# An MLP's up-projection as seven block products in place of eight, and its two halves split at DRAM

## The chip, the cores and the metric

The kernel runs on one core of one Trainium2 chip (trn2). TensorE (PE) multiplies, VectorE (DVE), ScalarE (ACT) and GpSimd (POOL) work on rows, and SyncE (SP) issues the transfers between DRAM and the on-chip memory SBUF. Products land in PSUM, in banks of 128 partitions x 512 float32. The metric is the time of one execution on the device, in microseconds (us).

## The reference, cut to what matters

```python
for i in range(DEPTH):                       # DEPTH = 2 layers
    ...                                      # four attention groups, h = h + mix @ w_o[i]
    hn = rms_norm(h, ffn_norm[i])            # 1024 tokens x 1024
    u = dwconv_centred(hn @ w_up[i], conv_w[i], conv_b[i])   # 1024 x 5632, 3 taps along the tokens
    gate, val = jnp.split(u, 2, axis=-1)
    h = h + (jax.nn.gelu(gate) * val) @ w_down[i]            # 2816 -> 1024
    e = p[i] @ w_ple_proj[i]
    g = jax.nn.sigmoid(rms_norm(h, ple_norm[i]) @ w_ple_gate[i])
    h = h + g * e
```

## The kernel before, in words

Every large product is made in three matmuls: both operands are split into a high part (a cast to the matmul's own float format, `hi`) and the rest (`lo`), and hi·hi, hi·lo and lo·hi are added up in PSUM (`products`, `mm3`, `mm_side`; the matmuls themselves are recorded at line L181). A split costs one cast and one subtraction over the same elements.

Per layer, around the change:

- **The projection stage** (`proj`, `turn`, `emb`), for each of 8 blocks of 128 tokens: the last half of the output projection is added to h, the rows are normed, transposed and split into `xh`/`xl` (two halves of 512 tokens), and e is made and stored to DRAM. All eight blocks of h stay in SBUF.
- **The MLP loop.** The 5632 columns of w_up lie in 44 tiles of 128; tile f (gate) and tile 22 + f (value) make one of the 22 activations. `up_tile` makes one tile: 48 matmuls 128x512 into `psS`, a pair of PSUM banks (two such pairs exist), then the three taps of the convolution straight out of PSUM (L1124 on ACT, L1125 and L1126 on DVE). `act_tile` calls it twice, puts gelu (L1133, ACT) and the product gate x value (L1135, POOL) behind it, and splits the result into `ah`/`al` (L1138 ACT, L1139 DVE). Activations never leave SBUF.
- Two activations make one chunk of the down-projection: `down_tile`, for each of the 8 token blocks, 12 matmuls into the two banks `psM(0)` and `psM(1)` and two additions to h on DVE (L1197). Eleven chunks. While chunk ch runs, the up tiles of chunk ch + 1 are made: a scheduler orders the instructions of each engine, and puts up matmuls between the down tiles.
- In the last layer (`last`) a down tile runs its two halves one after the other (`outs[:1]`, then `outs[1:]`); in the first layer it alternates between them.
- The last chunk of a layer (`down_last`) runs in a pipeline with the norm and the gate stage behind it. Its second activation is made in pieces by `act_last`.

Weights come as float32 tiles through `WRing.piece`: a transfer of 512 KB, and the split on POOL (L111 high part, L112 low part). Each engine works through its own queue in order; semaphores join them.

Of the kernel before, what the change touches and what calls it, by code (L numbers as in the profile page):

```python
# [19 lines left out]
P = 128  # L20
# [25 lines left out]
def kernel(ctx: ExitStack, tc: tile.TileContext, a, out, dbg=None):  # L46
# [992 lines left out]
    for L in range(DEPTH):  # L1039
# [10 lines left out]
        stg = c0.enter_context(tc.tile_pool(name="stg", bufs=2))  # L1050
        gp = c0.enter_context(tc.tile_pool(name="gp", bufs=1))
        hp = c0.enter_context(tc.tile_pool(name="hp", bufs=1))
        h = [hp.tile([P, D], F32, name=f"h{t}") for t in range(NT)]
        xF = [(xp.tile([P, KD, 512], F32R, name=f"xh{i}"), xp.tile([P, KD, 512], F32R, name=f"xl{i}"))
              for i in range(2)]

        with ExitStack() as c:
            mp = c.enter_context(tc.tile_pool(name="mp", bufs=2))
            np_ = c.enter_context(tc.tile_pool(name="nrm", bufs=2))
            ringe = WRing(c, "e", 6, 0, stage=ring.s)  # L1060
            ep = c.enter_context(tc.tile_pool(name="es", bufs=2))
            W = [ring.piece(a["w_o"][L, k * P:(k + 1) * P, :], 1024, pool=False) for k in (2, 3)]
            gB = load_gB(gp, a["ffn_norm"][L])
            Pt = [ringe.piece(a["p"][L, k * P:(k + 1) * P, :], 1024, pool=k == 0) for k in range(2)]
            We = {}

            def emb(i):
                n, t = i // NT, i % NT
                cs = slice(n * 512, (n + 1) * 512)
                if t == 0:  # L1070
                    We[n] = ringe.piece(a["w_ple_proj"][L, :, cs], 1024, 2)
                tf = slice(t * P, (t + 1) * P)
                e = psT(i)
                mm3(e, [((Pt[k][0][:, tf], Pt[k][1][:, tf]),
                         (We[n][0][:, k * 512:(k + 1) * 512], We[n][1][:, k * 512:(k + 1) * 512])) for k in range(2)])
                es = ep.tile([P, 512], F32, name="es", tag="es")
                se.copy(es, e)
                nc.sync.dma_start(ed[t][:, cs], es)

            def proj(t, _):  # L1080
                nc.sync.dma_start(h[t], hpart[t])
# [5 lines left out]
                for n in range(2):  # L1087
                    o = psM(n)
                    cs = slice(n * 512, (n + 1) * 512)
                    mm3(o, [((mh[:, k], ml[:, k]), (W[k][0][:, cs], W[k][1][:, cs])) for k in range(2)])  # L1090
                    ve.tensor_tensor(h[t][:, cs], o, h[t][:, cs], op=ALU.add)
                return norm_a(np_, h[t], gB)

            def turn(t, hn):
                tk = slice((t % 4) * P, (t % 4 + 1) * P)
                norm_b(hn, xF[t // 4][0][:, :, tk], xF[t // 4][1][:, :, tk], t if t < 4 else 1)
                emb(2 * t)
                emb(2 * t + 1)
# [4 lines left out]
        ap_ = cf.enter_context(tc.tile_pool(name="act", bufs=5))  # L1103
        kp = cf.enter_context(tc.tile_pool(name="cw", bufs=1))
        cw = kp.tile([P, 2 * NF, 4], F32, name="cw")
        nc.sync.dma_start(cw, a["conv"][L])
        cu = ExitStack()
        up_ = cu.enter_context(tc.tile_pool(name="up", bufs=2))

        def up_mm(f, dst):  # L1110
            hi, lo = ring.piece(a["w_up"][L, f], 1024)
            outs = [(dst[n], [((hi[:, k * P:(k + 1) * P], lo[:, k * P:(k + 1) * P]), (xF[n][0][:, k], xF[n][1][:, k]))
                              for k in range(KD)]) for n in range(2)]
            if last:
                for o, pairs in outs:
                    mm3(o, pairs, by_pass=True)
            else:
                mm_side(outs)

        def up_tile(f):  # L1120
            s = psS(0 if f < NF else 1)
            up_mm(f, (s[:, :512], s[:, 512:]))
            u = up_.tile([P, S], F32, name="u", tag="ug" if f < NF else "uv", bufs=2 if f < NF else 1)
            se.activation(u, s, AF.Identity, bias=cw[:, f, 3:4], scale=cw[:, f, 1:2])  # L1124
            ve.scalar_tensor_tensor(u[:, 1:], s[:, :S - 1], cw[:, f, 0:1], u[:, 1:], op0=ALU.mult, op1=ALU.add)  # L1125
            ve.scalar_tensor_tensor(u[:, :S - 1], s[:, 1:], cw[:, f, 2:3], u[:, :S - 1],  # L1126
                                    op0=ALU.mult, op1=ALU.add)
            return u

        def act_tile(f):  # L1130

            g = up_tile(f)
            se.activation(g, g, AF.Gelu_apprx_tanh)  # L1133
            v = up_tile(NF + f)
            ge.tensor_tensor(v, g, v, op=ALU.mult)  # L1135
            hi = ap_.tile([P, S], F32R, name="ah", tag="act")
            lo = ap_.tile([P, S], F32R, name="al", tag="act")
            se.copy(hi, v)  # L1138
            ve.tensor_tensor(lo, v, hi.bitcast(F32), op=ALU.subtract)  # L1139
            return lambda t: (hi[:, t * P:(t + 1) * P], lo[:, t * P:(t + 1) * P])  # L1140

        def act_last(f):

            g = up_tile(f)
            se.activation(g, g, AF.Gelu_apprx_tanh)
            f += NF
            s = (psT(0), psT(1))
            up_mm(f, s)
            cut = 384
            A = up_.tile([P, S], F32, name="u", tag="uv", bufs=1)[:, :cut]  # L1150
            B = up_.tile([P, S], F32, name="u", tag="ug", bufs=2)[:, :S - cut]

            def tap(u, o, src, j):
                ve.scalar_tensor_tensor(u[:, o:o + src.shape[1]], src, cw[:, f, j:j + 1],
                                        u[:, o:o + src.shape[1]], op0=ALU.mult, op1=ALU.add)

            def split(u, lo_):
                n = u.shape[1]
                ve.tensor_tensor(u, g[:, lo_:lo_ + n], u, op=ALU.mult)
                if lo_ == 0:  # L1160
                    x = ap_.tile([P, S], F32R, name="ahl", tag="act")
                    hi, lo = x[:, :n], x[:, n:2 * n]
                else:
                    hi = ap_.tile([P, S], F32R, name="ah", tag="act")[:, :n]
                    lo = ap_.tile([P, S], F32R, name="al", tag="act")[:, :n]
                se.copy(hi, u)
                ve.tensor_tensor(lo, u, hi.bitcast(F32), op=ALU.subtract)
                return hi, lo

            b, w = cw[:, f, 3:4], cw[:, f, 1:2]  # L1170
            se.activation(A, s[0][:, :cut], AF.Identity, bias=b, scale=w)
            tap(A, 1, s[0][:, :cut - 1], 0)
            tap(A, 0, s[0][:, 1:cut + 1], 2)
            pa = split(A, 0)
            m = 512 - cut
            se.activation(B[:, :m], s[0][:, cut:], AF.Identity, bias=b, scale=w)
            se.activation(B[:, m:], s[1], AF.Identity, bias=b, scale=w)
            tap(B, 0, s[0][:, cut - 1:511], 0)
            tap(B, m, s[0][:, 511:], 0)
            tap(B, m + 1, s[1][:, :511], 0)  # L1180
            tap(B, 0, s[0][:, cut + 1:], 2)
            tap(B, m - 1, s[1][:, :1], 2)
            tap(B, m, s[1][:, 1:], 2)
            pb = split(B, cut)

            def get(t):
                (hi, lo), o = (pa, t * P) if t * P < cut else (pb, t * P - cut)
                return hi[:, o:o + P], lo[:, o:o + P]
            return get

        def down_tile(t, acts, W):
            halves = [(psM(n), slice(n * 512, (n + 1) * 512)) for n in range(2)]
            outs = [(o, [(x(t), (wh[:, cs], wl[:, cs])) for x, (wh, wl) in zip(acts, W)]) for o, cs in halves]
# [5 lines left out]
        NC_ = NF // 2  # L1199
        pend = [act_tile(0), act_tile(1)]  # L1200
        for ch in range(NC_):
            W = [ring.piece(a["w_down"][L, f * P:(f + 1) * P, :], 1024) for f in (2 * ch, 2 * ch + 1)]
            cur = pend
            if ch + 1 == NC_:
                break
            pend = [act_tile(2 * ch + 2)]
            for t in range(NT):
                down_tile(t, cur, W)
            pend.append((act_last if ch + 2 == NC_ else act_tile)(2 * ch + 3))
        cu.close()  # L1210


        xt_cm.__exit__(None, None, None)
# [26 lines left out]
        with ExitStack() as c:  # L1240
# [5 lines left out]
            def down_last(t, _):  # L1246
                down_tile(t, cur, W)
# [108 lines left out]
```

## Time and profile before

| | before |
|---|---|
| median of 3 runs | 3514.02 us (3509.81 to 3517.78) |
| the profiled execution | 3509.35 us |
| its span, first to last instruction | 3507.3 us |
| mean granted clock of TensorE | 0.982 |
| PE busy | 3330.8 us, 95% of the span |
| DVE, ACT, POOL busy | 48%, 31%, 32% |

The span lies 2 us below the profiled execution's own time, and that execution 4.7 us below the median. A row of the profile gives an engine's busy time, a share of the span or the time of one instruction; a matmul's own duration overlaps the next one's, so the pace of a run of matmuls is read from the starts.

### The profile page before, as it was taken

The page shows a single profiled execution, that of the slowest core. Times are in us where ns is not written, and L with a number is a line of the kernel's source. Part 1 is how long each engine was busy: PE and PEld are TensorE (multiplying, and loading weights), DVE is VectorE, ACT ScalarE, POOL GpSimd, SP SyncE. Part 2 cuts the span into 40 slices and gives each one's busy share as a digit, 9 for nine tenths or more (in the row PEclk, how much of TensorE's full clock was granted, in tenths as well). Part 3 has the DMA queues.
Part 4 walks back from the last instruction along what each step waited for, and adds up shares of the span by engine and source line. Part 5 has one row for each costly group of instructions (what it writes and reads, how often), then busy time and mean ns, then how long its engine had stood idle before and what let it go on. Part 6 is the DMA issues. An engine that isn't in the chain of part 4 may idle for free.

```text
span 3507.3 us, 49133 instructions
## 1 busy us (share of the span) xinstructions
PE 3330.8 (95%) x19616; PEld 2762.2 (79%) x19616; DVE 1673.3 (48%) x2496; ACT 1103.0 (31%) x2188; POOL 1107.0 (32%) x1060
## 2 busy tenths in 40 slices
PE   8999889997999999999999998899979999999998
PEld 8888778775777777777998887777757888888888
DVE  5676346544333333335647763565442333333354
ACT  3554357533211111112225543564332111111122
POOL 1532213202333433442415332131033344343331
PEclk9999989998999999999999999999989999999999
DMA  6211322324211111111322113223242111111112
GB/s 195 82 55 53 101 82 79 111 80 156 79 48 37 57 46 42 55 48 39 125 97 65 54 53 105 82 79 116 76 157 79 43 54 44 47 48 48 49 50 95
DMA packets 170835, 264.09 MB, mean 75 GB/s; under 512 B 33008, under 2 KB 121968, under 8 KB 170608
## 3 DMA queue, kind: packets, MB, share of 16 engines
q1 hardware_dynamic: 170608, 260.96, 23.4%
q8 instruction: 155, 2.54, 0.3%
q14 instruction: 72, 0.59, 0.1%
HBM read 200.80 MB, written 63.77 MB: 75 GB/s over the span
## 4 chain that ended last, share of the span: by engine, by line
PE 77%; issue 6%; DVE 5%; POOL 5%; ACT 3%; DMA 3%; SPq 1%; POOLq 0%; ACTq 0%; DVEq 0%
PE psS L181 30%; PE psM L181 29%; PE psT L181 4%; PE psT L256 3%; PE psM L264 2%; POOL wlo L112 2%; PE psM L580 2%; PE psS L700 1%; PE psS L422 1%; DVE Prow L428 1%; PE psT L890 1%; DVE nm L279 1%; ACT Prow L281 1%; POOL whi L111 1%; PE psS L161 1%
## 5 line engine op out<-in xcount | busy, mean ns | idle before, releaser
L111 POOL TENSOR_SCALAR whi<-wst 128x1024 fp32r<-128x1024 f32 (+2 forms) x194 | 212.6, 1096 | 1105.6 <-PE psM L181 558.7
L112 POOL TENSOR_TENSOR wlo<-wst,whi 128x1024 fp32r<-128x1024 f32 (+2 forms) x194 | 480.2, 2475 | 51.2 <-PE psS L181 38.5
L1125 DVE SCALAR_TENSOR_TENSOR u<-psS,cw,u 128x1023 f32<-128x1023 f32 x86 | 110.3, 1283 | 619.1 <-ACT u L1124 619.1
L181 PE MATMUL psS<-xl,whi 128*128 128x512 f32 x1376 | 396.7, 394 | 0.0
L181 PE MATMUL psS<-xh,whi 128*128 128x512 f32 x1376 | 393.3, 394 | 0.0
L181 PE MATMUL psS<-xh,wlo 128*128 128x512 f32 x1376 | 390.2, 394 | 0.0
L1124 ACT ACTIVATE u<-psS,cw 128x1024 f32<-128x1024 f32 x86 | 104.0, 1209 | 873.1 <-PE psS L181 873.1
L181 PE MATMUL psM<-whi,xh 128*128 128x256 f32 (+1 forms) x1408 | 370.3, 301 | 0.1
L181 PE MATMUL psM<-whi,xl 128*128 128x256 f32 (+1 forms) x1408 | 360.7, 295 | 2.3 <-DVE xl L163 2.3
L181 PE MATMUL psM<-wlo,xh 128*128 128x256 f32 (+1 forms) x1408 | 358.1, 293 | 3.9 <-POOL wlo L112 3.9
L1197 DVE TENSOR_TENSOR h<-psM,h 128x512 f32<-128x512 f32 x352 | 235.2, 687 | 214.7 <-PE psM L181 214.7
L181 PEld LDWEIGHTS psS<-xh,wlo 128*128 128x128 f32 x1376 | 257.4, 187 | 63.5
L181 PEld LDWEIGHTS psS<-xl,whi 128*128 128x128 f32 x1376 | 257.4, 187 | 63.5
L181 PEld LDWEIGHTS psS<-xh,whi 128*128 128x128 f32 x1376 | 257.4, 187 | 62.9
L281 ACT ACTIVATE Prow<-psS,nm 128x1024 f32<-128x1024 f32 x192 | 214.4, 1118 | 195.8 <-DVE nm L279 195.3
L181 PE MATMUL psM<-whi,ah 128*128 128x512 f32 x692 | 264.6, 403 | 1.2 <-DVE h L1197 1.2
L181 PE MATMUL psM<-wlo,ah 128*128 128x512 f32 x692 | 256.4, 391 | 0.0
L181 PE MATMUL psM<-whi,al 128*128 128x512 f32 x692 | 255.9, 391 | 0.0
L181 PEld LDWEIGHTS psM<-whi,xh 128*128 128x128 f32 x1408 | 248.3, 193 | 7.9 <-ACT pr_raw L232 4.3
L279 DVE TENSOR_REDUCE nm<-psS 128x1 f32<-128x1024 f32 x192 | 230.5, 1216 | 47.6 <-PE psS L422 29.4
L181 PEld LDWEIGHTS psM<-wlo,xh 128*128 128x128 f32 x1408 | 248.5, 193 | 5.5 <-POOL wlo L112 5.4
L181 PEld LDWEIGHTS psM<-whi,xl 128*128 128x128 f32 x1408 | 248.9, 194 | 3.3 <-DVE xl L163 3.2
(276 smaller groups left out, 6001.9 us busy)
## 6 DMA issues: line engine op xcount, KB each, us to landing
wst<-w_up SPq DMA_DIRECT2D x88, 512.0 KB, 3.5
wst<-w_down SPq DMA_DIRECT2D x44, 512.0 KB, 3.3
wst<-w_in SPq DMA_DIRECT2D x36, 512.0 KB, 3.7
wst<-w_o SPq DMA_DIRECT2D x16, 512.0 KB, 4.4
hp<-o_hx SPq DMA_DIRECT2D x16, 512.0 KB, 2.6
h<-hp SPq DMA_DIRECT2D x16, 512.0 KB, 5.7
e<-es SPq DMA_DIRECT2D x32, 256.0 KB, 2.5
wst<-w_ple_gate SPq DMA_DIRECT2D x16, 512.0 KB, 3.5
```

The lines of the kernel that those rows point to most:

```text
L111: ge.tensor_scalar(hi, src, 1.0, 0.0, op0=ALU.mult, op1=ALU.add)
L112: ge.tensor_tensor(lo, src, hi.bitcast(F32), op=ALU.subtract)
L161: te.transpose(t[:, j], src[:, (c + j) * P:(c + j + 1) * P], ident)
L181: te.matmul(o, *ms[i], start=i == 0, stop=i == n - 1)
L256: te.transpose(t[:, i], src[:, (4 * c + i) * P:(4 * c + i + 1) * P], ident)
L264: te.matmul(o[z, :256], V(kt), PT[:, kt], start=(kt < 2), stop=(kt >= 6))
L279: ve.tensor_reduce(nm, s, op=ALU.max, axis=AX.X, negate=True)
L281: se.activation(p_, s, AF.Exp, bias=nm[:, 0:1], scale=1.0, accum_out=ssum)
L580: te.matmul(o[64 * j:64 * j + 64, g], V(2 * g + j, b), pt(2 * g + j, b), start=(b == 0), stop=(b == nb - 1))
L1124: se.activation(u, s, AF.Identity, bias=cw[:, f, 3:4], scale=cw[:, f, 1:2])
L1125: ve.scalar_tensor_tensor(u[:, 1:], s[:, :S - 1], cw[:, f, 0:1], u[:, 1:], op0=ALU.mult, op1=ALU.add)
L1197: ve.tensor_tensor(h[t][:, cs], o, h[t][:, cs], op=ALU.add)
```

## The change

The up-projection of one gate tile and its value tile is one product of a 2x2 block matrix of weights (gate and value by the two halves of the 1024 inputs; a11, a12, a21, a22) with a 2x2 block matrix of rows (b11, b12, b21, b22: the two halves of the inputs by the two halves of the tokens). It is made by Strassen's scheme in its form with fifteen additions: seven block products of 12 matmuls 128x512 in place of eight. The sums of the weights (s1 to s4) are made on POOL for each f, those of the rows (t1 to t4) once per layer in the projection stage. Three PSUM banks take the products: A is `psT`, B and C are the two halves of one `psS`. The results G and V are put together in SBUF by seven evictions, and the taps of the convolution read them there. The activation v goes to DRAM. When all 22 are done, h (stored to DRAM by the projection stage) is loaded again, and the down-projection runs alone: v is loaded, split and multiplied, in both layers with the two halves alternating. `act_last` is gone.

```diff
-        ring = WRing(c0, "f", 10, 2)
+        ring = WRing(c0, "f", 8, 4)
+        XC = ("b11", "b21", "b22", "t1", "t2", "t3", "t4")
...
-            def proj(t, _):
-                nc.sync.dma_start(h[t], hpart[t])
+            def proj(i, _):
+                t = tok(i)
+                ht = row_tile("h")
+                nc.sync.dma_start(ht, hpart[t])
...
+                nc.sync.dma_start(hd1[t], ht)
+                hn = row_tile("hn")
+                norm_rows(ht, gB, hn)
...
+                def split(name, src, e):
+                    hi, lo = (x[:, :, tk] for x in xc[name])
+                    se.copy(hi, src)
+                    e.tensor_tensor(lo, src, hi.bitcast(F32), op=ALU.subtract)
+                es = row_tile("es")
...
+                    ve.tensor_tensor(t1, b12, f[:, :4], op=ALU.subtract)
+                    ve.tensor_tensor(t2, s[:, 4:], t1, op=ALU.subtract)
+                    split("t2", t2, ge)
...
+        ap_ = c0.enter_context(tc.tile_pool(name="act", bufs=7))
+        sp_ = cu.enter_context(tc.tile_pool(name="wsum", bufs=4))
...
+        ORDER = (("a11", "b11", 0), ("s2", "t2", 1), ("a12", "b21", 0), ("s3", "t3", 1), ("s1", "t1", 2),
+                 ("a22", "t4", 1), ("s4", "b22", 2))
...
+                wsum(f, "s1", stat[f, "a21"], stat[f, "a22"], ALU.add)
+                wsum(f, "s2", stat[f, "s1"], stat[f, "a11"], ALU.subtract)
...
+            src = stat[f, ORDER[p][0]]
+            w = ring.w.tile([P, 1024], F32R, name="whl", tag="wp")
+            hi, lo = w[:, :512], w[:, 512:]
+            se.copy(hi, src)
+            (ve if p % 2 else ge).tensor_tensor(lo, src, hi.bitcast(F32), op=ALU.subtract)
...
+        def conv(f, u, x, half=None):
+            if half != 1:
+                se.activation(u, x, AF.Identity, bias=cw[:, f, 3:4], scale=cw[:, f, 1:2])
+                ve.scalar_tensor_tensor(u[:, 1:], x[:, :S - 1], cw[:, f, 0:1], u[:, 1:], op0=ALU.mult, op1=ALU.add)
+            if half != 0:
+                ve.scalar_tensor_tensor(u[:, :S - 1], x[:, 1:], cw[:, f, 2:3], u[:, :S - 1],
+                                        op0=ALU.mult, op1=ALU.add)
...
+            ge.tensor_tensor(v, g, v, op=ALU.mult)
+            nc.sync.dma_start(vd[f], v)
...
+        def act_load(f):
+            v = ring.s.tile([P, 1024], F32, name="wst")
+            nc.sync.dma_start(v, vd[f])
+            hi, lo = act("ah", F32R), act("al", F32R)
+            se.copy(hi, v)
+            ve.tensor_tensor(lo, v, hi.bitcast(F32), op=ALU.subtract)
...
+            s = psS(f)
+            banks = psT(f), s[:, :512], s[:, 512:]
...
+                multiply(f, p, banks)
+                if p == 0:
+                    se.copy(V[:, :512], A)
+                elif p == 1:
+                    ve.tensor_tensor(G[:, 512:], B, V[:, :512], op=ALU.add)
+                elif p == 2:
+                    se.copy(G[:, :512], A)
+                elif p == 3:
+                    ve.tensor_tensor(V[:, 512:], B, V[:, :512], op=ALU.add)
+                elif p == 4:
+                    ve.tensor_tensor(V[:, 512:], C, V[:, 512:], op=ALU.add)
...
+        for t in range(NT):
+            nc.sync.dma_start(h[t], hd1[t])
...
-            for z in ([outs[:1], outs[1:]] if last else [outs]):
-                mm_side(z)
+            mm_side(outs)
             for o, cs in halves:
                 ve.tensor_tensor(h[t][:, cs], o, h[t][:, cs], op=ALU.add)
...
+        for ch in range(NC_ - 1):
+            for t in range(NT):
+                down_tile(t, ch)
+                if t in (0, 2):
+                    act_load(2 * ch + 2 + t // 2)
+                elif t in (1, 3):
+                    down_w(2 * ch + 2 + t // 2)
```

The first place is DVE's queue in the up-projection. Before, in the steady part of the first layer, it held for each up tile two taps out of `psS`, and for each activation one subtraction for `al`:

```order
L1125 SCALAR_TENSOR_TENSOR u<-psS,cw,u 128x1023 [waits Activation_49]
L1126 SCALAR_TENSOR_TENSOR u<-psS,cw,u 128x1023 [waits DVE_49]
L1139 TENSOR_TENSOR al<-u,ah 128x1024 [waits Activation_49]
```

Now the queue holds for one f, from one L1198 to the next, the taps of the f before (`ug`, `uv`), the low parts of weights (`whl`, L1182) and the evictions of this f (L1245 after product 1, L1249 after 3, L1251 after 4, L1253 after 5, L1255 after 6):

```order
L1198 SCALAR_TENSOR_TENSOR ug<-G,cw,ug 128x1023 [waits Activation_49]
L1245 TENSOR_TENSOR G<-psS,V 128x512 [waits PE_49]
L1200 SCALAR_TENSOR_TENSOR ug<-G,cw,ug 128x1023 [waits DVE_49]
L1198 SCALAR_TENSOR_TENSOR uv<-V,cw,uv 128x1023 [waits Activation_49]
L1200 SCALAR_TENSOR_TENSOR uv<-V,cw,uv 128x1023 [waits DVE_49]
L1182 TENSOR_TENSOR whl<-wsum,whl 128x512 [waits PE_49,Activation_49]
L1249 TENSOR_TENSOR V<-psS,V 128x512 [waits DMAHW4_49,PE_49]
L1251 TENSOR_TENSOR V<-psS,V 128x512 [waits DVE_49,PE_49]
L1182 TENSOR_TENSOR whl<-wst,whl 128x512 [waits DMAHW5_49,Activation_49]
L1253 TENSOR_TENSOR V<-psS,V 128x512 [waits PE_49]
L1255 TENSOR_TENSOR G<-psS,G 128x512 [waits PE_49]
```

The taps have moved from PSUM to SBUF sources, and three of them and a low part now stand between the eviction L1245 and the eviction L1249.

PE's queue around the same eviction, in the same f: the end of product 3 (`t3`), four matmuls of the next f's product 0 (`b11`), and the start of product 4 (`t1`), whose wait is on L1249:

```order
L1193 MATMUL psS<-t3h,whl 128x512 x2
L1193 MATMUL psS<-t3l,whl 128x512
L1193 MATMUL psS<-t3h,whl 128x512
L1193 MATMUL psT<-b11h,whl 128x512 [waits Activation_49]
L1193 MATMUL psT<-b11l,whl 128x512
L1193 MATMUL psT<-b11h,whl 128x512 [waits Pool_49]
L1193 MATMUL psT<-b11h,whl 128x512
L1193 MATMUL psS<-t1h,whl 128x512 [waits DVE_49]
```

Product 4 goes to the other bank of the same `psS` tile that L1249 reads, and the wait is for the tile. Products 5 and 6 wait in the same way for L1251 and L1253, product 5 behind four matmuls of `b11`, product 6 behind four more.

The second place is PE's queue in the down-projection, at the border of two down tiles. Before, in the first layer, three matmuls of an up tile (`psS`) stood there:

```order
L181 MATMUL psM<-whi,ah 128x512 x2
L181 MATMUL psM<-wlo,ah 128x512 x2
L181 MATMUL psM<-whi,al 128x512 x2
L181 MATMUL psS<-xh_9318,whi 128x512
L181 MATMUL psS<-xh_9320,whi 128x512
L181 MATMUL psS<-xl_9319,whi 128x512
L181 MATMUL psM<-whi,ah 128x512 [waits DVE_49]
L181 MATMUL psM<-wlo,ah 128x512
```

Now, in both layers:

```order
L181 MATMUL psM<-whi,ah 128x512 x2
L181 MATMUL psM<-wlo,ah 128x512 x2
L181 MATMUL psM<-whi,al 128x512 x2
L181 MATMUL psM<-whi,ah 128x512 [waits DVE_49]
L181 MATMUL psM<-wlo,ah 128x512
L181 MATMUL psM<-whi,al 128x512
L181 MATMUL psM<-whi,ah 128x512 [waits DVE_49]
```

The matmul that waits for the addition to h now stands straight behind the last one of the tile before.

The third place is DVE's queue at the end of a chunk (h_13110 is block 6, h_13111 block 7, h_13104 block 0 of the next chunk). Before, one `al` stood there. Now there are two, which wait for matmuls of block 7 (`PE_49`), since the pool `act` has seven tiles for the eight that two chunks hold:

```order
L1285 TENSOR_TENSOR h_13110<-psM,h_13110 128x512 [waits DVE_49,PE_49] x2
L1229 TENSOR_TENSOR al<-wst,ah 128x1024 [waits DMAHW0_49,PE_49,Activation_49]
L1229 TENSOR_TENSOR al<-wst,ah 128x1024 [waits DMAHW4_49,DVE_49,DMAHW5_49,PE_49,Activation_49]
L1285 TENSOR_TENSOR h_13111<-psM,h_13111 128x512 [waits DVE_49,PE_49] x2
L1285 TENSOR_TENSOR h_13104<-psM,h_13104 128x512 [waits DVE_49,PE_49] x2
```

Both `al` have moved ahead of the additions of block 7.

## Rows read from the trace of the kernel before

**Rows 1.** The page: the engines' busy time, and the chain's shares by line.
```profile
PE 3330.8 (95%) x19616; PEld 2762.2 (79%) x19616; DVE 1673.3 (48%) x2496; ACT 1103.0 (31%) x2188; POOL 1107.0 (32%) x1060
PE psS L181 30%; PE psM L181 29%; PE psT L181 4%; PE psT L256 3%; PE psM L264 2%; POOL wlo L112 2%; PE psM L580 2%; PE psS L700 1%; PE psS L422 1%; DVE Prow L428 1%; PE psT L890 1%; DVE nm L279 1%; ACT Prow L281 1%; POOL whi L111 1%; PE psS L161 1%
```

**Rows 2.** Windows: projection stage, one chunk of layer 0, one of layer 1.
```profile
core 0: us, PE busy (x) PEld busy (x) DVE busy (x) ACT busy (x) POOL busy (x), PEclk, DMA share, GB/s
842.00:904.00 62.00, 52.00 (x245) 39.77 (x246) 32.92 (x35) 24.32 (x44) 28.64 (x29) 0.97 0.48 163
...
979.50:1047.30 67.80, 67.80 (x289) 53.38 (x289) 23.74 (x27) 9.05 (x8) 26.25 (x15) 1.00 0.14 45
...
2727.00:2793.70 66.70, 66.70 (x290) 53.88 (x289) 24.11 (x27) 9.05 (x8) 26.31 (x15) 1.00 0.15 47
```

**Rows 3.** The chain that ended last, layer 0, one chunk: start, us, what.
```profile
987.33 0.70 PE psS L181 x3
...
1001.75 39.90 PE psS L181 x171
```

**Rows 4.** The same chain, layer 1.
```profile
2727.02 17.70 PE psM L181 x78
```

**Rows 5.** Timeline of PE at a border of two down tiles, layer 0.
```profile
983.14 0.62 PE L181 MATMUL psM<-whi,al 128*128 128x512 f32 x2
983.59 0.63 PE L181 MATMUL psS<-xh,whi 128*128 128x512 f32 x2
...
984.31 0.51 PE L181 MATMUL psM<-whi,ah 128*128 128x512 f32 x1
```

**Rows 6.** Timeline of DVE at that border and the next.
```profile
983.57 1.29 DVE L1197 TENSOR_TENSOR h<-psM,h 128x512 f32<-128x512 f32 x2 [1.97 <-PE psM L181]
987.14 1.29 DVE L1197 TENSOR_TENSOR h<-psM,h 128x512 f32<-128x512 f32 x2 [2.29 <-PE psM L181]
```

**Rows 7.** Groups by line and shape: xcount | busy us, mean ns.
```profile
L1197 DVE TENSOR_TENSOR h<-psM,h 128x512 f32<-128x512 f32 x352 | 235.2, 687 | 214.7 <-PE psM L181 214.7
L1125 DVE SCALAR_TENSOR_TENSOR u<-psS,cw,u 128x1023 f32<-128x1023 f32 x86 | 110.3, 1283 | 619.1 <-ACT u L1124 619.1
L450 POOL TENSOR_TENSOR c_ob<-oh,gsub 128x512 f32<-128x512 f32 x8 | 10.3, 1288 | 0.6
L1135 POOL TENSOR_TENSOR u<-u 128x1024 f32<-128x1024 f32 x42 | 100.5, 2394 | 59.1 <-DVE u L1126 59.1
L1124 ACT ACTIVATE u<-psS,cw 128x1024 f32<-128x1024 f32 x86 | 104.0, 1209 | 873.1 <-PE psS L181 873.1
L1077 ACT COPY es<-psT 128x512 f32<-128x512 f32 x32 | 18.4, 583 | 11.9 <-DMA e<-es 7.1 <-ACT es L1077 2.5 <-PE psT L181 2.2
L658 DVE TENSOR_TENSOR a_sl<-a_x,a_sh 128x512 fp32r<-128x512 f32 x16 | 11.0, 688 | 3.4 <-ACT a_sh L657 2.9 <-DMA a_V<-A 0.5
```

**Rows 8.** Timelines of POOL and DVE: `al` beside POOL's split, and alone.
```profile
1001.35 3.24 POOL L112 TENSOR_TENSOR wlo<-wst,whi 128x1024 fp32r<-128x1024 f32 x1
...
1005.69 2.39 POOL L112 TENSOR_TENSOR wlo<-wst,whi 128x1024 fp32r<-128x1024 f32 x1
...
1000.24 2.10 DVE L1139 TENSOR_TENSOR al<-u,ah 128x1024 fp32r<-128x1024 f32 x1 [0.99 <-PE psM L181]
...
1026.78 1.23 DVE L1139 TENSOR_TENSOR al<-u,ah 128x1024 fp32r<-128x1024 f32 x1 [3.65 <-ACT ah L1138]
```

**Rows 9.** The chain ahead of the last chunk, layer 0.
```profile
1628.93 0.03 issue
...
1633.36 1.41 PE psM L181 x5
```

**Rows 10.** The page: DMA issues, KB each, median us to landing.
```profile
hp<-o_hx SPq DMA_DIRECT2D x16, 512.0 KB, 2.6
h<-hp SPq DMA_DIRECT2D x16, 512.0 KB, 5.7
```

**Rows 11.** The longest wait in the projection stage, layer 0: us, times, longest.
```profile
ACT xh L162 <- PE psS L161: 26.5, 7, 10.1
```

More of the change, by code (lines that the diff above doesn't have):

```diff
@@ L1048 @@
         c0 = ctx.enter_context(ExitStack())
-        ring = WRing(c0, "f", 10, 2)
[L1050 to L1055, printed above, removed]
+        ring = WRing(c0, "f", 8, 4)
@@ L1062, with row_tile @@
             W = [ring.piece(a["w_o"][L, k * P:(k + 1) * P, :], 1024, pool=False) for k in (2, 3)]
             gB = load_gB(gp, a["ffn_norm"][L])
-            Pt = [ringe.piece(a["p"][L, k * P:(k + 1) * P, :], 1024, pool=k == 0) for k in range(2)]
+            Pt = [ring.piece(a["p"][L, k * P:(k + 1) * P, :], 1024, pool=k == 0) for k in range(2)]
             We = {}
-            def emb(i):
-                n, t = i // NT, i % NT
+            def row_tile(name):
+                return np_.tile([P, D], F32, name=name, tag="row")
@@ new lines, in multiply @@
+        def multiply(f, p, banks):
+            hi, lo = stat.pop((f, p))
+            _, x, z = ORDER[p]
+            xh, xl = xc[x]
+            ms = products([((hi[:, k * P:(k + 1) * P], lo[:, k * P:(k + 1) * P]), (xh[:, k], xl[:, k]))
+                           for k in range(4)])
+            first = [o[2] for o in ORDER].index(z) == p
+            for i, m in enumerate(ms):
+                te.matmul(banks[z], *m, start=first and i == 0, stop=i == len(ms) - 1, skip_group_check=True)
+        def conv(f, u, x, half=None):
[5 more added lines that the diff above has]
+                                        op0=ALU.mult, op1=ALU.add)
@@ new lines, in down_w @@
+        def down_w(f):
+            Ws[f] = ring.piece(a["w_down"][L, f * P:(f + 1) * P, :], 1024)
+        for f in range(NF):
+            s = psS(f)
+            banks = psT(f), s[:, :512], s[:, 512:]
+            A, B, C = banks
+            G, V = act("G"), act("V")
+            for p in range(7):
+                multiply(f, p, banks)
+                if p == 0:
+                    se.copy(V[:, :512], A)
[7 more added lines that the diff above has]
+                    ve.tensor_tensor(V[:, 512:], C, V[:, 512:], op=ALU.add)
+                elif p == 5:
+                    ve.tensor_tensor(V[:, :512], B, V[:, :512], op=ALU.add)
+                else:
+                    ve.tensor_tensor(G[:, 512:], C, G[:, 512:], op=ALU.add)
+                if f + 1 < NF:
+                    prep(f + 1, p)
+                elif p in (1, 2):
+                    down_w(p - 1)
+                elif p in (4, 5):
+                    act_load(p - 4)
+                if p == 0 and f + 2 < NF:
+                    raw_load(f + 2)
+                next(rest, None)
+            rest = hidden(f, G, V)
@@ L1101 @@
+        for _ in rest:
+            pass
+        cu.close()
+        xt_cm.__exit__(None, None, None)
+        stg = c0.enter_context(tc.tile_pool(name="stg", bufs=2))
+        gp = c0.enter_context(tc.tile_pool(name="gp", bufs=1))
+        hp = c0.enter_context(tc.tile_pool(name="hp", bufs=1))
+        h = [hp.tile([P, D], F32, name=f"h{t}") for t in range(NT)]
+        for t in range(NT):
+            nc.sync.dma_start(h[t], hd1[t])
         cf = ExitStack()
         np_ = cf.enter_context(tc.tile_pool(name="nrm", bufs=2))
-        ap_ = cf.enter_context(tc.tile_pool(name="act", bufs=5))
@@ L1104 @@
[L1104 to L1118, printed above, removed]
@@ L1142, in act_last @@
[L1142 to L1189, printed above, removed]
```

132 lines of the change are left out of this document (84 added, 48 removed).

## The prediction

> **What bounds the kernel now.** I read the page's busy times first, then the chain that ended last, then windows cut at the chain's own period, then timelines inside one period. TensorE is busy for 95% of the span, and the two matmul lines of the MLP make most of the chain [rows 1]. The window of one chunk shows PE busy for all of it in either layer, at a granted clock of 1.00, while DVE works some 24 us of 67 and POOL 26 [rows 2]. So in the MLP every matmul taken out is worth its pace, as long as no new wait appears, and every wait put on PE costs its length.
>
> The pace comes from the chain, which joins matmuls that follow each other without a gap. Up-projection: 39.90 us for 171, 0.2333 us each [rows 3]. Down-projection in layer 1, with halves one after the other: 17.70 us for 78, 0.2269 us [rows 4]. The down tiles of layer 0 need a closer look. Three up matmuls, 0.70 us, stand between two tiles [rows 3]. The last pair of a tile starts at 983.14, the addition to h starts at 983.57 and takes 1.29 us for two halves, so the first half is free at about 984.2, and the next tile's first matmul starts at 984.31 [rows 5, 6]. PE was ready for it at 983.59, when it started the first of the three fillers [rows 5]. The eviction therefore costs a wait of 0.72 us, and the fillers hide it, no more and no less. In layer 1 the second half's matmuls hide it, which is why that layer needs no fillers.
>
> **Part 1, the up-projection.** One f takes 7 x 12 = 84 matmuls in place of 2 x 48 = 96. At 0.2333 us that is 19.6 us in place of 22.4; over 22 f 431 in place of 493 us; for two layers a gain of **123 us**. This is the ceiling.
>
> Added are weight sums and low parts on POOL (eight 128x512 operations at 1.29, one product at 2.39: 12.7 us per f), seven casts, two copies, two taps and a gelu on ACT (nine at 0.58 and three at 1.2: 8.8), and on DVE four taps, three low parts and five additions (4 x 1.23, 3 x 0.69, 5 x 0.69: 10.4 us) [rows 7, 8]. None reaches 19.6, so no engine's sum becomes the bound. The order does: product 4 waits for L1249, in front of which stand three taps and a low part, after L1245, which has to wait for product 1.
>
> Count from the end of product 6. Product 1 ends 12 matmuls later, at 2.8; L1245 at 3.5; three taps of 1.23 to 7.2; the low part to 7.9. L1249 also needs product 3, at 8.4, so it would be done at 9.15, and product 4, which PE reaches at 40 matmuls or 9.33, would not wait. That holds if each DVE step takes its time alone. The trace speaks against it. `al` has two SBUF inputs, and took 2.10 beside POOL's split and 1.23 alone; POOL's L112 took 3.24 and 2.39 [rows 8]. They shut each other out: both ends lie later by about the other's piece. Before, the taps read PSUM and kept 1.283 us over all 86 [rows 7]. Now they, too, have two SBUF inputs, and POOL is at work two thirds of the time. One or two collisions with a 1.29 us operation, or the product of 2.39 us against the low part (both are released by the fourth tap), put L1249's end at 10.5 to 13. Bounds for the wait per f: 0, and 4.1 (each of the four steps loses a whole 1.29 us operation: 7.9 + 5.2 + 0.7 = 13.8, less 9.33, less some that POOL hasn't ready). Products 5 and 6 have four fillers, 0.93 us, to hide an eviction of 0.69 and its semaphores (0.72 above), so they wait little. I take **1.6 us per f**, nearer to the lower bound because the collisions before L1245 cost nothing: 44 x 1.6 = +70, bounds 0 and +180.
>
> The Trainium skill has the rule behind this in "SBUF — State Buffer", section "Who interferes with whom": a DVE instruction with two SBUF inputs and a GpSimd instruction that reads SBUF want the same port pair, and the second to come is blocked until the first ends; one with at most one SBUF input doesn't contend. It speaks against moving the taps from PSUM to SBUF; the durations above agree with it. Without it this term would be 0, with it +70.
>
> **Part 2, the down-projection alone.** Nothing is left to fill the 0.72 us. The period from one tile's additions to the next was 983.57 to 987.14, 3.57 us, fillers included [rows 6]; the chain last matmul, addition, next tile's first matmul doesn't contain the fillers, so it stays at 3.57 without them. Before, the chunk's own matmuls cost 67.80 - 192 x 0.2333 = 23.0 us in layer 0 and 66.70 - 44.8 = 21.9 in layer 1 [rows 2]. Now 8 x 3.57 = 28.6. Ten chunks each (the last runs between the norm and gate stages as before): 56 + 67 = **+123 us**, bounds +110 and +130. What was saved in part 1 is given back here.
>
> At the end of each chunk two subtractions for `al` stand on DVE ahead of block 7's additions. They wait for matmuls of block 7 and for the casts, and the weight splits on POOL are released by the same matmuls. Alone they hold the additions up by about one operation, 1.23, less some slack; shut out by POOL twice (2.10 as in [rows 8], and more against 2.39) by up to 4.5. Lower bound 0.4. I take **2.5 us**, twice the duration alone: 20 chunk ends, +50, bounds +8 and +90. The transfers of v and the weights (four of 512 KB in 29 us, a few us each [rows 10]) are asked for a chunk ahead and are hidden.
>
> **The borders.** Between up and down, h has to be loaded: a transfer of 512 KB lands in 2.6 to 5.7 us [rows 10], the first addition needs one, and two tiles can't run ahead of it: +3 per layer, bounds 0 and 6. At the end `act_last` is gone: in the chain before, PE stood from 1628.93 to 1633.36 for its taps [rows 9]: -4.4 per layer. Together -3.
>
> **The projection stage.** It took 62.0 us, PE busy for 52 [rows 2], and the longest of its waits is ACT's for the transposes, 26.5 us, which PE doesn't feel [rows 11]. Added per pair of blocks: four differences and five more splits of 512 columns, and five shared row buffers in place of eight h and two hn, so that a block's h and sums wait for earlier stores. The matmuls stay. The extra DVE work is some 16 operations of 0.69, 11 us, on 33; POOL's 16 low parts of 1.29, 21 us, on 29 [rows 2, 7]. Below: hidden, 0. Above: POOL's and half of DVE's come on top, +30. I take **+15** per layer, +30.
>
> **Sum.** -123 + 70 + 123 + 50 - 3 + 30 = +147, on the profiled execution's 3509: 3656; against the median, which lies 5 us higher, **3661 us**.
>
> **Rivals.**
> - *The ports bind the up loop* (chance 0.14). Each tap loses a POOL operation: wait near 4.1 per f, +110 over mine, about 3770. For it: POOL's 65% busy share. Against: POOL's product waits for the fourth tap, so POOL is idle for part of the stretch.
> - *The up loop runs at its matmuls' pace* and only the down part waits (0.14): 3661 - 70, about 3590. For it: the walk without collisions ends 0.2 us before PE needs the bank.
> - *An even exchange* (0.06): only the 0.72 us wait is real, `al` and the projection stage hide: 3514 - 123 + 123, about 3514.
> - *PE finds the banks free* (0.06, the other side): DVE keeps up wherever PE asks. Place: the border of two down tiles and the border of products 3 and 4; price: 123 + 70 + 50 less; result some 3420. It decides if an eviction ends within the time that PE needs to come back to its bank; at the down border that time is nothing and the eviction 0.65 us, so little speaks for it.
> - Mine: 0.60. That the seven products don't save 12 matmuls per f is ruled out by the order.
>
> **How the numbers follow.** The bounds of the terms, added as independent ones (70, 42, 30 and 12 down; 110, 40, 30 and 10 up), give 3661 - 88 and + 121. The range reaches a little past the low rival at 3590 and to the port rival: **3555 to 3780**; it leaves out the last two rivals and the tails, 0.2. My own case alone: 3600 to 3725. A difference of 0.2%, 7 us, is what a measurement here can tell from no change. Faster: 0.06 and a share of the even exchange, 0.08; same 0.03; slower 0.89.
>
> **What the profile after would show.** PE's busy share in the up windows under 1, with PE waiting for DVE L1249, a period of 20.5 to 22 us per f, and taps with means over 1.23. In the down windows a period near 3.57 per tile with PE waiting for L1285, about 31 us per chunk, the longest wait of a chunk at its end behind L1229. No up matmul in the down part. The prediction is wrong if down tiles follow each other in under 3 us, if L1249 is done before PE gets there, or if the projection stage takes over 95 us.

## The result, and the profile after

The changed kernel takes **3665.64 us** (median of 4 runs, 3657.91 to 3667.94) against 3514.51 for the kernel before: a ratio of 1.0427, 95% interval 1.0408 to 1.0447. The profiled execution's span is 3656.1 us at a mean granted clock of 0.971; before it was 3507.3 at 0.982. So 148.8 us have to be found between the two spans.

The page's part on busy time answers to [rows 1]: PE does 528 matmuls fewer (12 for each of the 44 f), 37 us of busy time less, and its share falls from 95% to 90%.

```profile
PE 3293.3 (90%) x19088; PEld 2668.5 (73%) x19088; DVE 1975.8 (54%) x2874; ACT 1352.4 (37%) x2630; POOL 1349.0 (37%) x1262
```

What PE waits for, in all and in the whole span (engine and line, whom for, us, times, longest us):

```profile
PE psM L181 <- DVE h L1285: 134.5, 160, 5.6
PE psS L1108 <- DVE t L1131: 26.4, 6, 4.8
PE psS L1193 <- DVE V L1249: 26.2, 40, 1.1
...
PE psS L1193 <- DVE whl L1182: 10.0, 2, 5.0
```

The first row is the down-projection, the third the up-projection, the second the projection stage, and each is a place that the change made. Windows of four f of the up-projection and of one chunk of the down-projection, both layer 0, answer to [rows 2]:

```profile
core 0: us, PE busy (x) PEld busy (x) DVE busy (x) ACT busy (x) POOL busy (x), PEclk, DMA share, GB/s
987.49:1070.45 82.96, 80.37 (x337) 62.24 (x336) 45.58 (x48) 34.63 (x48) 54.36 (x37) 1.00 0.23 77
1452.24:1482.79 30.55, 24.22 (x96) 17.39 (x97) 13.39 (x19) 2.10 (x2) 8.76 (x5) 1.00 0.21 69
```

An f takes 82.96 / 4 = 20.74 us; a chunk, 96 matmuls in either kernel, takes 30.55 where the chunk before spent 23.0 and 21.9 us on it. The granted clock is 1.00 in both windows, as before. Timelines of the three engines show the two waits themselves, first in the up-projection, then at the end of a chunk:

```profile
1030.70 1.32 POOL L1159 TENSOR_TENSOR wsum<-wst 128x512 f32<-128x512 f32 x1 [0.70 <-POOL whl L1182]
1032.67 1.59 POOL L1182 TENSOR_TENSOR whl<-wst,whl 128x512 fp32r<-128x512 f32 x1 [0.65 <-ACT whl L1181]
1038.01 2.69 POOL L1212 TENSOR_TENSOR uv<-ug,uv 128x1024 f32<-128x1024 f32 x1 [3.74 <-DVE uv L1200]
...
1031.24 1.87 DVE L1198 SCALAR_TENSOR_TENSOR ug<-G,cw,ug 128x1023 f32<-128x1023 f32 x1 [0.67 <-ACT ug L1197]
1033.03 0.68 DVE L1245 TENSOR_TENSOR G<-psS,V 128x512 f32<-128x512 f32 x1
1033.63 1.72 DVE L1200 SCALAR_TENSOR_TENSOR ug<-G,cw,ug 128x1023 f32<-128x1023 f32 x1
1035.27 1.27 DVE L1198 SCALAR_TENSOR_TENSOR uv<-V,cw,uv 128x1023 f32<-128x1023 f32 x1
1036.58 1.28 DVE L1200 SCALAR_TENSOR_TENSOR uv<-V,cw,uv 128x1023 f32<-128x1023 f32 x1
1037.78 0.68 DVE L1182 TENSOR_TENSOR whl<-wsum,whl 128x512 fp32r<-128x512 f32 x1
1038.38 0.68 DVE L1249 TENSOR_TENSOR V<-psS,V 128x512 f32<-128x512 f32 x1
...
1039.12 0.50 PE L1193 MATMUL psS<-t1h,whl 128*128 128x512 f32 x1 [0.65 <-DVE V L1249]
...
1478.84 3.20 DVE L1229 TENSOR_TENSOR al<-wst,ah 128x1024 fp32r<-128x1024 f32 x2 [1.00 <-issue]
1481.97 1.27 DVE L1285 TENSOR_TENSOR h<-psM,h 128x512 f32<-128x512 f32 x2
...
1477.31 0.50 PE L181 MATMUL psM<-whi,ah 128*128 128x512 f32 x1 [0.56 <-DVE h L1285]
...
1482.79 0.47 PE L181 MATMUL psM<-whi,ah 128*128 128x512 f32 x1 [2.45 <-DVE h L1285]
```

In the first half, DVE goes from the first tap to L1249 without a pause; the two that lie beside a POOL operation take 1.87 and 1.72, the two that don't 1.27 and 1.28; L1249 ends at 1039.06 and product 4 starts at 1039.12, 0.8 us behind PE's pace. This is so in 40 of the 44 f. In the second, both `al` stand ahead of block 7's additions, and PE waits 2.45 us in place of 0.56.

### The profile page after: what moved, and what is told of

It is laid out like the page before. It is cut to its first block, busy times and chain, and to the rows that moved or that the text cites. A ratio compares the mean times of both kernels' runs of the same rounds, so it can differ in the third digit from the quotient of the medians.

```text
span 3656.1 us, 50036 instructions
## 1 busy us (share of the span) xinstructions
PE 3293.3 (90%) x19088; PEld 2668.5 (73%) x19088; DVE 1975.8 (54%) x2874; ACT 1352.4 (37%) x2630; POOL 1349.0 (37%) x1262
## 5 line engine op out<-in xcount | busy, mean ns | idle before, releaser
L111 POOL TENSOR_SCALAR whi<-wst 128x1024 fp32r<-128x1024 f32 (+2 forms) x102 | 139.6, 1369 | 727.4 <-PE psM L181 636.9
L1285 DVE TENSOR_TENSOR h<-psM,h 128x512 f32<-128x512 f32 x352 | 226.3, 684 | 326.3 <-PE psM L181 326.1
L181 PE MATMUL psM<-whi,ah 128*128 128x512 f32 x704 | 268.1, 425 | 135.8 <-DVE h L1285 134.5
L181 PEld LDWEIGHTS psM<-whi,ah 128*128 128x128 f32 x704 | 134.1, 192 | 231.9 <-DVE h L1285 150.2
L112 POOL TENSOR_TENSOR wlo<-wst,whi 128x1024 fp32r<-128x1024 f32 (+2 forms) x102 | 259.5, 2544 | 21.0 <-PE psS L1193 11.3
L1228 ACT CAST ah<-wst 128x1024 fp32r<-128x1024 f32 x44 | 46.1, 1048 | 517.4 <-PE psM L181 494.6
L1181 ACT CAST whl<-wsum 128x512 fp32r<-128x512 f32 x176 | 108.8, 621 | 237.9 <-PE psS L1193 216.5
L1212 POOL TENSOR_TENSOR uv<-ug,uv 128x1024 f32<-128x1024 f32 x44 | 116.7, 2652 | 169.4 <-DVE uv L1200 162.0
L256 PE MATMUL psT<-identr,Prow 128*128 128x128 f32 x1024 | 150.2, 278 | 16.7 <-DVE Prow L428 11.1
L256 PEld LDWEIGHTS psT<-identr,Prow 128*128 128x128 f32 x1024 | 115.3, 141 | 62.7 <-issue 28.1
L181 PEld LDWEIGHTS psM<-whi,al 128*128 128x128 f32 x704 | 134.6, 191 | 33.6 <-DVE al L1229 2.7
L1181 ACT CAST whl<-wst 128x512 fp32r<-128x512 f32 x132 | 82.0, 622 | 200.1 <-PE psS L1193 194.7
```

What stands on the lines that cost most here:

```text
L111: ge.tensor_scalar(hi, src, 1.0, 0.0, op0=ALU.mult, op1=ALU.add)
L112: ge.tensor_tensor(lo, src, hi.bitcast(F32), op=ALU.subtract)
L181: te.matmul(o, *ms[i], start=i == 0, stop=i == n - 1)
L256: te.transpose(t[:, i], src[:, (4 * c + i) * P:(4 * c + i + 1) * P], ident)
L1181: se.copy(hi, src)
```

## The experiments

Unless it says otherwise, each edits the changed kernel, and is compared with it.

**1. The halves of a down tile one after the other** (what layer 1 had before).

```diff
-            mm_side(outs)
+            for z in (outs[:1], outs[1:]):
+                mm_side(z)
```

> Down tiles run their two halves one after the other in both layers; the rest is the changed kernel. Theory A (the 0.72 us from the last matmul of a half, over its addition on DVE, to the next matmul of that bank stands open on PE): the period of a down tile falls from 3.60 to 2.73 us, 0.87 x 7 x 20 tiles and more, the whole about 120 to 140 us faster, some 3525 to 3545. The end of a chunk keeps a wait of 1 to 3 us behind the subtractions for al. Rival B (the down part is slow because its operands come from DRAM, or since the weights are split too late): the period stays above 3.4 us and the time above 3640.

Measured 3539.27 us (ratio to the kernel before 1.006, 1.0037 to 1.0083), 126 us faster than the changed kernel. One chunk, and PE's largest wait in the whole span:

```profile
1439.95:1464.62 24.67, 22.64 (x97) 17.87 (x96) 15.48 (x19) 2.01 (x3) 7.75 (x5) 1.00 0.25 86
```
```profile
PE psM L181 <- DVE h L1286: 41.2, 20, 5.6
```

The wait falls from 134.5 us over 160 waits to 41.2 over 20: one per chunk is left. The first tile of a chunk takes 5.5 us, the second 2.9, the other six 2.72. Theory A holds. Six tiles of eight run at the pace of their matmuls, 12 x 0.2269 us, so operands out of DRAM cost them nothing; at the border of two chunks a wait of some 2.8 us is left, behind the subtractions for `al`.

**2. Bank C in a tile of its own.**

```diff
-            banks = psT(f), s[:, :512], s[:, 512:]
+            banks = psT(f), s[:, :512], psM(f)
```

> In the up-projection bank C is a psM tile of its own and no longer the second half of the psS tile that holds B, so products 4 and 6 do not wait for evictions of B. Theory A (the wait for L1249 through the shared tile): the period per f falls from 20.74 to 19.6 to 19.8 us, 44 x 1.0 = 45 us faster, about 3615. Rival B (the three taps and low parts, shut out by POOL, set the pace of DVE whatever bank is used): the wait moves to product 5 and the period stays over 20.4, the time over 3645.

Measured 3625.93 us, 40 us faster. Four f, then L1249 and the start of product 5 in one of them:

```profile
1003.97:1083.52 79.55, 79.46 (x337) 62.81 (x336) 51.29 (x48) 34.17 (x48) 57.14 (x37) 1.00 0.23 80
```
```profile
1014.63 0.67 DVE L1249 TENSOR_TENSOR V<-psS,V 128x512 f32<-128x512 f32 x1
...
1015.36 0.50 PE L1193 MATMUL psS<-t4h,whl 128*128 128x512 f32 x1
```

19.89 us per f. DVE's busy time has grown (two taps per f now take 2.3 and 2.2 us beside POOL), and product 4 doesn't wait any more: the wait of 0.8 us came from two banks in one tile. A little of rival B is there too. Product 5 writes to the bank that L1249 reads; it starts 0.06 us behind L1249's end and 0.2 us behind PE's pace, and with 0.1 us at its second matmul that is the 0.3 us between 19.89 and 19.6. DVE's queue is close to its limit.

**3. `al` on POOL.**

```diff
-            ve.tensor_tensor(lo, v, hi.bitcast(F32), op=ALU.subtract)
+            ge.tensor_tensor(lo, v, hi.bitcast(F32), op=ALU.subtract)
```

> The subtraction for al in the down part runs on POOL in place of DVE. Theory A (two al stand ahead of block 7's additions in DVE's queue): the last tile of a chunk falls from 5.47 to about 3.6 us, and the chunk from 30.6 to 28.7 or a little more; 20 x 1.9 = 38 us faster, about 3625. Rival B (PE waits at the end of the chunk for the activations themselves, which come late because seven tiles hold them): POOL needs 2.4 us where DVE needed 1.2, the wait at the chunk's border stays or grows, the time is 3655 or more.

Measured 3625.43 us, 40 us faster. One chunk takes 28.60, eight tiles of 3.54 to 3.66:

```profile
1446.84:1475.44 28.60, 24.04 (x97) 17.40 (x97) 10.31 (x17) 2.11 (x3) 11.53 (x7) 1.00 0.23 74
```

Theory A holds: what was late was an addition behind `al` in a queue, not `al`.

**4. No weight sums on POOL.**

```diff
-            ge.tensor_tensor(r, x, y, op=op)
-            stat[f, name] = r
+            stat[f, name] = x
```

> The four weight sums per f on POOL are left out (the products take one of the two blocks as it is, so they are not the scheme's); PE's and DVE's operations and their order stay. Theory A (POOL's operations shut out the taps, and that makes L1249 late): POOL's busy time falls by 5 us per f, the mean of the taps falls from about 1.53 towards 1.27, and the period per f from 20.74 to 20.1 to 20.5. Rival B (DVE's own order makes L1249 late, POOL has no part in it): taps and period stay as they are, 20.7.

Measured once, 3639.76 us. Four f take 81.79, 20.45 us each. The taps, by line and tile (median in the middle), of this kernel, where they stand at L1196 and L1198, and then of the changed one:

```profile
L1196 DVE SCALAR_TENSOR_TENSOR ug<-G,cw,ug x44: 1283/1284/1537, 946.2 to 3184.6; 128x1023 f32<-128x1023 f32 x44
L1198 DVE SCALAR_TENSOR_TENSOR ug<-G,cw,ug x44: 1285/2009/2023, 948.0 to 3186.0; 128x1023 f32<-128x1023 f32 x44
```
```profile
L1198 DVE SCALAR_TENSOR_TENSOR ug<-G,cw,ug x44: 1284/1860/1873, 948.9 to 3199.7; 128x1023 f32<-128x1023 f32 x44
L1200 DVE SCALAR_TENSOR_TENSOR ug<-G,cw,ug x44: 1285/1718/2014, 951.3 to 3201.2; 128x1023 f32<-128x1023 f32 x44
```

The first tap, which lay beside a sum, is back at 1284 ns; the second now starts 0.37 us behind one of POOL's low parts and takes 2.01 us. The mean of the four falls only from 1.51 to 1.45 us. By the medians, what the two taps lose per f falls from 1.01 to 0.72 us, and the period by as much, 0.29 us, inside the range of theory A. POOL has a part in the wait; its low parts were still there, so this run doesn't say how much all of POOL would give.

**5. The three edits together**, with `al` on POOL for the first activation of a chunk and on DVE for the second.

> Three edits of the changed kernel together: halves one after the other in the down tiles, bank C in a psM tile of its own, and the subtraction for al on POOL for the first activation of a chunk and on DVE for the second. If the three waits are apart from each other: 3539 with the halves alone, less 39 for the bank, less 20 x 2 to 2.7 us at the ends of chunks, some 3445 to 3465, that is 1.4 to 2% under the kernel before. Rival (the waits overlap: where one goes another takes its place): 3490 or more.

Measured **3462.82 us** (3455.76 to 3465.98, 4 runs): a ratio to the kernel before of 0.9844, 0.9828 to 0.9861. Four f, one chunk, and PE's largest wait:

```profile
991.18:1070.77 79.59, 79.44 (x338) 62.86 (x337) 51.33 (x48) 34.17 (x48) 57.14 (x37) 1.00 0.24 80
1420.79:1443.46 22.67, 22.33 (x97) 17.94 (x96) 12.91 (x18) 2.01 (x3) 10.09 (x6) 1.00 0.29 94
```
```profile
PE psS L1108 <- DVE t L1131: 26.4, 6, 4.8
```

The waits are apart from each other: the gains of experiments 1 to 3, 126, 40 and 40 us, would add up to 3460. The chunk is 22.67 us, and the waits for L1285's additions and for L1249 are no longer PE's largest.

**6. The same with both `al` on POOL.**

> The same three edits, but both subtractions for al on POOL. POOL needs 2.4 us for each where DVE needs 1.2, and with the halves apart the last use of the first activation lies only 3 matmuls ahead of a tile's end: the second activation of the next chunk should come late at the chunk's border, 1 to 3 us each, so the time lies 20 to 40 us above that of the kernel with one of them on DVE, some 3470 to 3500. Rival (POOL has slack enough and the border stays free): within 5 us of it.

Measured 3468.71 us (3458.46 to 3472.57; ratio 0.9855, 0.9832 to 0.9877): 6 us above, not 20 to 40, and the ranges of the two kernels overlap. I had it wrong: a chunk takes 22.6 us, so POOL's 2.4 us come in time at the border. In the traces the first and the last chunk are longer (30.8 and 47.3 us in layer 1, against 28.5 and 45.0).

**7. The kernel before, with alternating halves in layer 1 too.**

```diff
-            for z in ([outs[:1], outs[1:]] if last else [outs]):
-                mm_side(z)
+            mm_side(outs)
```

> The kernel before, with the two halves of a down tile alternating in layer 1 as well; the scheduler puts three up matmuls between two tiles there too. Theory A (three up matmuls, 0.70 us, cover the wait of 0.72 us for the addition): the time stays within 0.3% of the kernel before. Rival B (alternating halves cost the wait with or without fillers): 88 tiles x 0.7, some 60 us slower.

Measured 3531.1 us (ratio 1.0042, 1.0027 to 1.0056): a little outside theory A's 0.3%, far from B's 60 us. The chain in layer 1 has layer 0's pattern, and one chunk 67.75 in place of 66.70:

```profile
2813.20 2.88 PE psM L181 x12
2816.08 0.70 PE psS L181 x3
```

Three fillers cover all but some 0.13 us of the wait per tile (1.05 / 8), so theory A has the cause, and its 0.3% was a little tight.

**8. The projection stage**, five kernels. The edits: t1 and t4 from the second block's PSUM pair (`f[:, :4]` and `f[:, 4:]` become `s[:, 4:]`); casts of t1 to t4 on POOL; eight row buffers. The stage begins with the first transposes of `mixt`, and two ends are used: the first matmul of the up-projection (in the changed kernel 85.9 us later in layer 0), and the first t2 product, the second of the seven (91.2 us).

> In the projection stage the differences t1 and t4 read the second block's PSUM pair in place of the first's, with the same number of operations of the same shape; so the first block's pair comes free at its splits, and t1 and t4 are not the scheme's. Theory A (the transposes of the next pair wait for the last difference, since both psS pairs are held): the three waits of 4 to 5 us per layer go for at least the even blocks, and the stage is 5 to 13 us shorter per layer, 10 to 25 us in all. Rival B (the added work on ACT, DVE and POOL sets the stage's pace): no change over 3 us per layer.

3667.07 us. PE's waits for L1131 are gone, and the stage is as long as it was: 86.5 us to the first up matmul in layer 0, 91.9 to the first t2 product. Waits for ACT's copies have taken the place; in the changed kernel they are 3.2 us in this window:

```profile
PE psT L161 <- ACT es L1077: 8.8, 3, 3.4
PE psT L181 <- ACT es L1077: 7.1, 3, 3.0
```

> The kernel with the three edits, and in the projection stage the four casts per pair for t1 to t4 run on POOL in place of ACT. Theory A (PE waits for the burst of ten ACT operations after the second block's transposes, ahead of the next block's cast): the stage, 86 us from its first transposes to the first product of the up-projection, is 4 to 8 us shorter per layer, the whole some 3450. Theory B (both psS pairs are held until the fourth difference, which does not depend on the casts): no change over 2 us per layer, 3460 to 3465. Theory C (POOL's casts and low parts shut out the differences on DVE): the stage is longer.

3473.39 us (ratio 0.9882, 0.9861 to 0.9903), 11 us above experiment 5: to the first t2 product the stage takes 98.2 us where that kernel's takes 92.2, to the first up matmul 88.6 against 86.9. PE's wait for the fourth difference stays at 13.2 us a layer. Theory A falls. The stage is longer, as theory C says, but not for its reason: in layer 0 all 16 differences take 0.68 or 0.69 us, as they did. What grows is PE's wait for the weights of the second product, 6.6 us where it was 2.2.

> The changed kernel with both taken out of the way: t1 and t4 read the second block's PSUM pair (so they are not the scheme's) and the four casts per pair run on POOL. If the stage's 12 us per layer come from the hold of the pair and from ACT's burst, either of which covers the other, the stage falls from 86 to some 75 to 80 us per layer, and the time by 12 to 20 us. If neither is it (row buffers, the added work as such), the stage stays at 84 us or more.

Measured once, 3658.4 us. To the first up matmul the stage takes 82.5 us in layer 0 and 83.1 in layer 1, 3.4 less than in the changed kernel and between the two cases that were forecast; to the first t2 product 92.1, as before.

> The changed kernel with eight row buffers in the projection stage in place of five; the space comes from t4, which shares its buffer with t3 (so one product of the seven takes the wrong rows). From its first transposes to the first t2 product that follows a full product the stage took 91 us. Theory A (the five shared row buffers set the pace: loads of h wait for late readers): 80 to 86 us. Theory B (both psS pairs are held until the fourth difference): the stage stays within 2 us, and PE's waits for it stay at 13 us per layer.

Measured once, 3664.6 us; the stage 86.7 us to the first up matmul and 95.4 to the first t2 product. The wait for the fourth difference falls to 1.2 us, which theory B didn't expect, and the stage is no shorter, which theory A didn't. Both fall.

> Eight row buffers, and also t1 and t4 from the second block's PSUM pair and the four casts per pair on POOL: all three suspects are taken out. If they cover each other: 91 us fall below 84. If the stage still takes 89 us or more, its pace is set by the chain of one block after the other (addition, norm, transposes, splits) or by the split of the first weights, and not by buffers.

Measured once, 3660.59 us; the stage 80.9 us to the first up matmul and 90.9 to the first t2 product. Two waits of its window, and what stands ahead of the t2 product:

```profile
PE psT L161 <- ACT es L1078: 10.5, 3, 3.9
PE psS L1197 <- ACT whl L1185: 7.0, 1, 7.0
```
```profile
922.50 1.26 POOL L1163 TENSOR_TENSOR wsum<-wsum,wst 128x512 f32<-128x512 f32 x1
...
923.80 0.62 ACT L1185 CAST whl<-wsum 128x512 fp32r<-128x512 f32 x1 [2.12 <-POOL wsum L1163]
...
924.47 0.80 PE L1197 MATMUL psS<-t2h,whl 128*128 128x512 f32 x1 [6.99 <-ACT whl L1185]
```

With all three suspects out the stage is 5.0 us shorter to its first up matmul, but as long as it was to the second product (90.9 where it was 91.2). This is the forecast's second case, and of its two reasons the split of the first weights shows. The second product needs the sum s2, which POOL makes in its queue behind work for t1 to t4 (in the changed kernel too: s2 at 916.77, its cast at 918.07, the product at 918.74). So the end of the stage hangs on POOL's queue, to which the casts add work. A kernel that makes the first sums earlier wasn't run, and which link of the chain from one block to the next sets the pace before that stays open.

## Why the prediction held, step by step

3661 was forecast, 3665.6 came out. The direction and the three waits came as forecast. That the sum lies so close is luck: its terms were off by up to 44 us, and made up for each other. Between the spans, 148.8 us: the two MLPs, from the first up matmul to the start of the last down matmul, +134.1 us (layer 0 from 769.6 to 828.2, layer 1 from 755.4 to 830.9), the projection stages to their first up matmul +24.1 (73.4 to 85.9, and 74.8 to 86.4), the rest -9.4. The rest lies ahead of the projection stages, which begin 5.6 us earlier and follow layer 0's last down matmul 5.4 us sooner. No term stood for it, and the kernels of the experiments differ there as much among themselves (the first stage begins between 826.1 and 837.4).

- *Seven products*: 84 matmuls per f at the forecast pace of 0.2333 us; with bank C apart the f takes 19.89, near the 19.6 of the sum. That is 2.5 us under the 22.4 of before, or 110 of the 123 us of the ceiling.
- *The wait for L1249*: 1.6 us per f forecast, 20.74 - 19.6 = 1.14 measured, 50 us in place of 70. Product 4 waits 0.8 of it; the rest is 0.11 us at the start of each of the products 4, 5 and 6. The place was right, and so was the cause: DVE's operations collide with POOL's. The walk to it was not. It let L1245 end 3.5 us after the end of product 6 and held collisions ahead of it to be free. But a tap stands ahead of L1245 in the queue, and starts only when L1255, the eviction of product 6, and ACT's part of the convolution (L1197) are done:

```profile
1028.97 0.39 PE L1193 MATMUL psS<-t2h,whl 128*128 128x512 f32 x1
...
1029.17 0.69 DVE L1255 TENSOR_TENSOR G<-psS,G 128x512 f32<-128x512 f32 x1 [3.16 <-PE psS L1193]
...
1029.96 1.24 ACT L1197 ACTIVATE ug<-G,cw 128x1024 f32<-128x1024 f32 x1
```

  Counted from 1028.97, where product 1 starts, L1245 ends at 4.7 and L1249 at 10.1 (forecast: 9.15 without collisions, 10.5 to 13 with them). The collision of that first tap, 0.60 us, therefore counts in full, and of the three taps behind L1245 only one collided (1.72, 0.45 us more than alone). The rule of the Trainium skill ("SBUF — State Buffer", "Who interferes with whom") agrees with these rows in which operations lose: taps with two SBUF inputs do, L1245 and L1249 with one don't (0.68 beside POOL). In how much they lose the rows differ from it: by the rule the second to come is blocked until the first ends, and the first tap lost 0.60 us of the 0.78 that POOL still took; the measured loss stands. What makes the collision cost time is that product 4's bank shares a tile with the bank that L1249 reads: in experiment 2 the taps lose 2.0 us per f, and product 4 feels nothing. The same rows put the low part ahead of POOL's product at the fourth tap; the other order, which I priced, didn't come up there.
- *The eviction's wait per down tile*: 0.72 us from [rows 5, 6], a period of 3.57 forecast, 3.56 to 3.61 measured in nearly all tiles. Experiment 1 takes it away and gets 126 us back; experiment 7 shows from the kernel before that three up matmuls had hidden it, but for 0.13 us.
- *`al` at the end of a chunk*: 2.5 us forecast, 1.9 measured (a last tile of 5.47 in place of 3.57), and behind four of the chunks another 1.4 to 2.2 us at the next first tile. Experiment 3 gets 40 us back, of the 50 forecast.
- *The borders*: this step failed in size. I had -3 us. The MLPs' 134.1 less the steady f (2 x (22 x 20.74 - 493) = -73) and nine chunks per layer (276.4 against 207, and 277.0 against 197) leave +58, of which the forecast for the first chunks and borders was some 14. PE waits 5.0 and 2.3 us for the first weights at the start of each up loop, which I had at nothing. From the last up matmul to the second chunk it takes 35.3 and 37.3 us, where seven tiles of 3.6 and the 1.9 make 27.1 (the eighth lies between the last up products): here the first additions to h stand in DVE's queue behind taps of the last f, and PE waits 5.6 us for them. And the last chunk takes 45 us where it took 43, so the 4.4 us of `act_last` are half given back.
- *The projection stage*: 15 us forecast, 12 measured per layer. The reason that I gave, row buffers, is not borne out (experiment 8). The stage's 272 matmuls keep PE busy for 66.9 and 67.4 us where it was 61.0 and 62.6, at a granted clock of 0.85 and 0.82 in place of 0.93 and 0.90. The lower clock comes with the longer waits; how much of the 12 us it makes isn't shown.

Of the rivals, that PE finds the banks free failed at the border of two down tiles, as the price from one timeline said. The even exchange let only that border's wait be real; it failed since the wait for L1249, `al`, the borders and the stage weren't hidden. That the ports bind (3770) failed too: the taps lose 1.0 us per f, and the 2.0 us of experiment 2 still fit into 19.89. The rival in which only the down part waits (3590) is what experiment 2 should have given; it gave 3626, and the difference is the borders above all.

## What to carry to other kernels

Ahead of cutting matmuls, look for what they cover: a chain from the last matmul of a bank over its eviction to the bank's next matmul costs next to nothing as long as enough other products stand between, and comes back in full where two passes are pulled apart. The cheapest cure is in the order: let the halves of a tile run one after the other, so that one covers the other's eviction, and give each product that must not wait a PSUM tile of its own. An operation that frees nobody shouldn't stand in an in-order queue ahead of an eviction; here it went to an engine with time to spare. With these three edits the changed kernel is 1.6% faster than the kernel before. The same caution holds for the cure: in an in-order queue, work that is moved to an idle engine stands ahead of whatever comes next there, as POOL's casts did ahead of the first weight sums.

## What the runs showed of the hardware that I had not expected

A collision between DVE and POOL doesn't cost a whole operation of the other: a tap of 1.27 us that starts 0.54 us behind a POOL sum of 1.32 takes 1.87, so it loses 0.60 us of the 0.78 that were left of the sum. And POOL's product, when DVE came first by 0.23 us with an operation of 0.68, took 2.69 to 2.39 alone. The loss depends on the offset, and the same two queues, period after period, kept the same offset: in 38 of the 44 f the first tap starts 0.52 to 0.54 us behind the sum and takes 1.85 to 1.87 us; the other six, at the ends of the loops, meet other operations or none.
